# Second branch projection with eight of sixteen k-tiles as seven products for eight, modulation block 5 in the scan's last part, three low parts of y by adding DMAs

## The chip, the cores and the metric

The kernel runs on one core of a Trainium2 chip. The metric is the device time of one execution in microseconds (us), the median of three runs.

## What is computed

One step of a hybrid encoder layer for two groups of requests, 512 prompt frames and 64 sample frames, which share all weights (T = 576 rows together). The layer has a sparse attention branch and a Mamba-2 branch; each is projected back to 1024 channels and gated, the sum goes through an output projection, and a SwiGLU feed-forward part follows. The part that the change is about:

```
mod = (jax.nn.silu(c) @ w_ada + b_ada)[:, None, :]
sh1, sc1, gt1, sh2, sc2, gt2 = jnp.split(mod, 6, axis=-1)
...
y = (y.astype(x.dtype) + d_skip[:, None] * xh).reshape(b, t, D_INNER) * jax.nn.silu(z)
y = rms_normalize(y.reshape(b, t, SSM_GROUPS, D_INNER // SSM_GROUPS)).reshape(b, t, D_INNER) * g_ssm_norm
g_attn, g_ssm = jnp.split(jax.nn.sigmoid(gate_logits), 2, axis=-1)
mixed = (g_attn * (o_attn @ w_branch_attn) + g_ssm * (y @ w_branch_ssm)) @ w_out
x = x + gt1 * mixed
h2 = rms_normalize(x) * g_norm_ffn * (1.0 + sc2) + sh2
```

`o_attn` has 1024 columns, `y` has 2048. `w_ada` has 6 x 1024 columns; the kernel works on it in 12 blocks of 512 columns, and block u gives half of the u // 2-th of the six vectors (4 and 5: gt1; 6 and 7: sh2; 8 and 9: sc2; 10 and 11: gt2).

## The kernel before

**Numbers.** Every float32 operand of a large product is split into a high part (rounded to the format that TensorE multiplies fast, "float32r") and a low part, the rest. A product is hi·hi + hi·lo + lo·hi, three matmuls. ScalarE writes the high part (`wh`, `yh`, `mh`), VectorE subtracts it for the low part (`wl`, `yl`, `ml`). In 23 places GpSimd does it by an adding DMA instead: ScalarE writes the negative of the high part, and the DMA adds the raw value onto it (`split`, `by_dma`).

**Layout.** Activations lie with channels on the 128 partitions and the 576 rows in the free dimension, in two halves of TH = 288 (256 prompt rows and 32 sample rows in later stages). One matmul multiplies a 128 x 128 weight tile with 128 x 288 activations. A column block is 128 output channels. PSUM has the tag `mm` (two tiles of two banks), `px` and `py` (two banks each).

**Order of stages.** Input projection, attention, the scan of the Mamba-2 branch over eight channel groups g (`stage_a`, `stage_b`, `stage_c`), first branch projection (`pba`, eight column blocks of 8 k-tiles, attention), second branch projection (`pbs`, eight column blocks of 16 k-tiles, y), output projection (`pwo`), feed-forward part, of which most is computed with Strassen's method in Winograd's form: seven products of quarter matrices in place of eight, with sums of weight quarters (T1 to T4) and of activation quarters (S1 to S4).

**Scan, last part.** In the last groups the scan is a chain of short steps on all engines; matmuls of the first projection stand between them. `stage_c` of a group ends with y times its norm, written to DRAM (`y_d`), from which `load_split` (L1553) brings 128 x 576 tiles back into `stage` buffers and splits them. The last group's y stays in `ykeep`.

**Second projection** (L1620 to L1631). `gs` is the gate of a column block, `m` the gated first branch, which was written to DRAM (`m_d`). After the 96 matmuls of a block VectorE computes (gate + 1) times the product out of PSUM, adds `m`, ScalarE takes the high part `mh`, VectorE the low part `ml`, which the output projection reads.

**Modulation.** `ada_columns` (L792) multiplies 512 columns of `w_ada` with the two conditioning vectors on VectorE: per block 2 instructions of one operand, 14 that also add (tile `aacc`), on four loads of 512 KB (`adr`). `ada_sum` then adds over the partitions with 8 small matmuls and a transpose. Blocks 5 to 9 stand with low priority beside the second projection.

**What sets the order.** The kernel first records every operation and then a planner (`Plan.order`) puts them in order for each engine, by list scheduling: it has a cost for each kind of operation, buffers (`bufs`), priorities (`R.prio`, more is earlier) and a slack that it keeps between a producer and a matmul (`R.slack`). The engines then run that order strictly; an instruction whose input is late holds up all behind it on its engine, and SyncE's and GpSimd's DMA queues are such orders too. Weights are loaded (`raw`, 2 buffers) and split (3 buffers of `wh` and `wl`) ahead of their use by `fetch` (L628), and taken by `getw` (L657). All instructions have the line of the recording layer, so the profile is read by tile names.

Of the kernel before, what the change touches and what calls it, by code (L numbers as in the profile page):

```python
# [248 lines left out]
class Plan:  # L249
# [39 lines left out]
    def add(self, eng, fn, args, kw):  # L289
# [20 lines left out]
        op.dur, op.dur_dma = self.cost(op, outs, ins)  # L310
        self.ops.append(op)
# [240 lines left out]
def build(tc, I, O):  # L552
# [62 lines left out]
    queue = []  # L615
    state = {"ld": 0, "sp": 0, "get": 0}
    raws, outs, outs_made = {}, {}, []
# [9 lines left out]

    def fetch(done, limit=1 << 30):  # L628

        while len(outs_made) < len(specs):  # L630
            i = len(outs_made)
            outs_made.append(i)
            queue.extend((i, s) for s in specs[i])
            outs[i] = []
        with R.prio(4000 if done else 0):
            more = True
            while more:
                more = False
                j = state["ld"]
                if j < min(len(queue), limit) and j < state["sp"] + NRAW:  # L640
                    i, s = queue[j]
                    if s == "misc":
# [4 lines left out]
                    else:  # L647
                        raws[j] = (load_raw(*s), s[1], s[2], 27 <= j < 48)
# [3 lines left out]
                if j < min(state["ld"], limit) and (j < NWH or queue[j - NWH][0] < done):  # L652
                    outs[queue[j][0]].append(split(*raws.pop(j)))
                    state["sp"] += 1
                    more = True
# [87 lines left out]
    def ada(u, pl, bufs):  # L743

        p = px(f"pada{u}", "py")
        raws = [pl.tile([P, 2, 512], F32, name=f"wada{u}_{k2}", tag="adr", bufs=bufs) for k2 in range(4)]
        loads = [sync.dma_start(raw, w_ada[256 * k2:256 * k2 + 256, 512 * u:512 * u + 512].rearrange("(k p) n -> p k n", p=P))
                 for k2, raw in enumerate(raws)]
        with R.after(loads[-1:]):
            for kt in range(8):  # L750
                for g in range(4):
                    pe.matmul(p[32 * g:32 * g + 32, 0:P], sil[:, kt, :], raws[kt // 2][:, kt % 2, P * g:P * g + P],
                              start=(kt == 0), stop=(kt == 7), tile_position=(0, 32 * g))
        ada_out(u, p)

# [36 lines left out]
    def ada_columns(u, pl, nacc=1, bufs=2, nk=2, tags=None, late=False):  # L792

        acc = [pl.tile([P, 512], F32, name=f"aacc{u}{s}", tag=tags[s] if tags else f"aacc{s}", bufs=nacc) for s in range(2)]
        for k0 in range(0, 8, nk):
            raw = pl.tile([P, nk, 512], F32, name=f"wada{u}_{k0}", tag=tags[2 + k0 // nk % 2] if tags else "adr", bufs=bufs)
            (pool if u == 10 else sync).dma_start(raw, w_ada[P * k0:P * (k0 + nk), 512 * u:512 * u + 512].rearrange("(k p) n -> p k n", p=P))
            for j in range(nk):
# [8 lines left out]
        ada_sum(u, acc, px(f"padc{u}"))  # L807
# [550 lines left out]
    oh = [op_.tile([P, T], F32R, name=f"oh{k}") for k in range(8)]  # L1358
    ol = [op_.tile([P, T], F32R, name=f"ol{k}") for k in range(8)]
# [189 lines left out]
    def keep_split(o, hi, lo):  # L1549
        act.activation(hi, o, AF.Copy)  # L1550
        vec.tensor_tensor(lo, o, hi.bitcast(F32), OP.subtract)

    def load_split(pl, src, hi, lo, bufs):  # L1553
        o = pl.tile([P, T], F32, name="st_" + hi.base.name, tag="stage", bufs=bufs)
        sync.dma_start(o, src)
        keep_split(o, hi, lo)
# [701 lines left out]
```

## Time and profile before

| | us |
|---|---|
| median of three runs | 1356.81 (1356.64 to 1356.99) |
| profiled execution, its own time | 1357.67 |
| its span, first to last instruction | 1355.7 |

In a profile, each engine's busy time is counted from the start of its instructions to their end. PE is TensorE's matmuls, PEld its weight loads, DVE VectorE, ACT ScalarE, POOL GpSimd, SP SyncE. A group of instructions has a line `out<-in`, its shapes, count, busy time and mean nanoseconds, then the idle time of the engine just ahead of it and what ended that. In a list of waits the numbers are total, count and longest. A row of the chain has start, length, engine and tile. The busy shares in 40 slices of the run:

```profile
PE   7999999999999999999999999999999999999998
DVE  5788999887778798888887688867799999878897
ACT  5445333777777666666565342225476666665453
POOL 2312011230310235545463300001000000000000
DMA  9762435574755464454445698747423343325352
```

One slice is 33.9 us. The second branch projection lies in slices 24 to 27, where GpSimd has next to nothing to do and ScalarE is the least busy.

### The profile page before, as it was taken

The page shows a single profiled execution, that of the slowest core. Times are in us where ns is not written, and L with a number is a line of the kernel's source. Part 1 is how long each engine was busy: PE and PEld are TensorE (multiplying, and loading weights), DVE is VectorE, ACT ScalarE, POOL GpSimd, SP SyncE. Part 2 cuts the span into 40 slices and gives each one's busy share as a digit, 9 for nine tenths or more (in the row PEclk, how much of TensorE's full clock was granted, in tenths as well). Part 3 has the DMA queues.
Part 4 walks back from the last instruction along what each step waited for, and adds up shares of the span by engine and source line. Part 5 has one row for each costly group of instructions (what it writes and reads, how often), then busy time and mean ns, then how long its engine had stood idle before and what let it go on. Part 6 is the DMA issues. An engine that isn't in the chain of part 4 may idle for free.

```text
span 1355.7 us, 27900 instructions
## 1 busy us (share of the span) xinstructions
PE 1341.3 (99%) x10677; PEld 1306.5 (96%) x10677; DVE 1141.8 (84%) x2307; ACT 754.1 (56%) x1593; POOL 245.4 (18%) x377
## 2 busy tenths in 40 slices
PE   7999999999999999999999999999999999999998
PEld 6999999999999999999999999999999999999998
DVE  5788999887778798888887688867799999878897
ACT  5445333777777666666565342225476666665453
POOL 2312011230310235545463300001000000000000
PEclk9999999999999999999999999999999999999999
DMA  9762435574755464454445698747423343325352
GB/s 302 226 181 83 111 107 156 124 186 106 173 136 123 131 180 115 113 150 128 131 124 172 209 294 253 232 141 246 127 87 101 96 131 102 94 74 141 98 164 63
DMA packets 267877, 200.31 MB, mean 148 GB/s; under 512 B 25488, under 2 KB 239616, under 8 KB 267744
## 3 DMA queue, kind: packets, MB, share of 16 engines
q1 hardware_dynamic: 263056, 183.40, 46.3%
q0 software_dynamic: 4400, 15.00, 5.4%
q8 instruction: 83, 1.36, 0.4%
q14 instruction: 50, 0.41, 0.1%
q10 hardware_dynamic: 288, 0.13, 0.0%
HBM read 157.75 MB, written 28.96 MB: 138 GB/s over the span
## 4 chain that ended last, share of the span: by engine, by line
PE 91%; DVE 5%; DMA 1%; issue 1%; ACT 1%; POOL 1%; SPq 0%; DVEq 0%; POOLq 0%; ACTq 0%
PE mm L544 63%; PE py L544 16%; PE px L544 12%; DVE score L544 1%; DVE m L544 1%; DMA raw<-in_w_in 1%; DVE wl L544 1%; DMA bc<-acs_d 0%; DMA B<-in_w_down 0%; SPq L544 0%; DVE tok L544 0%; DVE xs L544 0%; ACT wh L544 0%; DVE rr L544 0%; ACT wl L544 0%
## 5 line engine op out<-in xcount | busy, mean ns | idle before, releaser
L544 ACT ACTIVATE wh<-raw 128x1024 fp32r<-128x1024 f32 (+3 forms) x144 | 140.6, 979 | 172.5 <-PE mm L544 131.6
L544 PE MATMUL mm<-hTl,wh 128*128 128x288 f32 (+1 forms) x1024 | 232.6, 302 | 1.1 <-DVE hTl L544 1.1
L544 PE MATMUL mm<-hTh,wh 128*128 128x288 f32 (+1 forms) x1024 | 231.2, 303 | 0.6 <-ACT wh L544 0.5
L544 PE MATMUL mm<-hTh,wl 128*128 128x288 f32 (+1 forms) x1024 | 230.0, 302 | 0.0
L544 PEld LDWEIGHTS mm<-hTl,wh 128*128 128x128 f32 (+1 forms) x1024 | 166.7, 188 | 4.1 <-DVE hTl L544 1.8
L544 PEld LDWEIGHTS mm<-hTh,wh 128*128 128x128 f32 (+1 forms) x1024 | 165.7, 188 | 3.8 <-ACT wh L544 0.7
L544 PEld LDWEIGHTS mm<-hTh,wl 128*128 128x128 f32 (+1 forms) x1024 | 165.4, 188 | 1.6 <-issue 0.9
L544 DVE TENSOR_TENSOR wl<-raw,wh 128x1024 fp32r<-128x1024 f32 (+2 forms) x99 | 122.1, 1235 | 27.1 <-ACT wh L544 26.0
L544 POOL DMA_DIRECT2D wl<-raw x23 | 20.9, 907 | 471.2 <-PE px L544 312.9
L544 DVE SCALAR_TENSOR_TENSOR cu<-xc,wc,cu 128x579 f32<-128x579 f32 x96 | 83.3, 868 | 2.0 <-ACT cu L544 1.0
L544 PE MATMUL mm<-wh,hTl 128*128 128x256 f32 x256 | 73.2, 286 | 0.0
L544 PE MATMUL mm<-wl,hTh 128*128 128x256 f32 x256 | 72.5, 284 | 0.0
L544 PE MATMUL mm<-wh,hTh 128*128 128x256 f32 x256 | 72.4, 285 | 0.0
L544 DVE SCALAR_TENSOR_TENSOR aacc<-adr,sil,aacc 128x512 f32<-128x512 f32 x84 | 59.0, 751 | 5.0 <-DMA adr<-in_w_ada 4.9
L544 PE MATMUL mm<-yh,wl 128*128 128x288 f32 x256 | 55.2, 296 | 0.0
L544 PE MATMUL mm<-yh,wh 128*128 128x288 f32 x256 | 55.0, 296 | 0.0
L544 PE MATMUL mm<-yl,wh 128*128 128x288 f32 x256 | 54.9, 296 | 0.0
L544 PE MATMUL mm<-xhS,wh 128*128 128x290 f32 (+1 forms) x248 | 54.8, 296 | 0.0
L544 ACT ACTIVATE P<-lg,mn 128x128 f32<-128x128 f32 (+4 forms) x72 | 41.7, 580 | 22.6 <-DVE mn L544 21.3
L544 ACT ACTIVATE dec<-dec,nacs 128x128 f32<-128x128 f32 x128 | 42.4, 393 | 15.9 <-POOL dec L544 15.9
L544 PE MATMUL mm<-xhS,wl 128*128 128x290 f32 (+1 forms) x232 | 51.2, 296 | 0.0
L544 PEld LDWEIGHTS mm<-wh,hTl 128*128 128x128 f32 x256 | 48.3, 189 | 0.4
(565 smaller groups left out, 4071.7 us busy)
## 6 DMA issues: line engine op xcount, KB each, us to landing
raw<-in_w_in SPq DMA_DIRECT2D x80, 512.0 KB, 4.2
adr<-in_w_ada SPq DMA_DIRECT2D x36, 512.0 KB, 5.4
raw<-in_w_gate_up SPq DMA_DIRECT2D x22, 512.0 KB, 3.8
wl<-raw POOLq DMA_DIRECT2D x21, 512.0 KB, 4.7
rawu<-in_w_gate_up SPq DMA_DIRECT2D x20, 512.0 KB, 3.9
bc<-acs_d SPq DMA_DIRECT2D x32, 256.0 KB, 3.7
raw<-in_w_branch_ssm SPq DMA_DIRECT2D x16, 512.0 KB, 4.7
gate_d<-sg SPq DMA_DIRECT2D x16, 288.0 KB, 2.2
```

What stands on the lines that cost most here:

```text
L544: getattr(engines[x.eng], x.fn)(*[real(a) for a in x.args], **{k: real(v) for k, v in x.kw.items()})
```

## The change

**Second projection.** Of y's 16 k-tiles the first eight (groups 0 to 3 of the scan) are cut in four quarters, by halves of the k-tiles and halves of the rows (A11, A12, A21, A22), and the weights of two neighbouring column blocks in quarters as well (B11 to B22). Such a pair of column blocks, here called a group r = 0 to 3, takes seven products of 4 k-tiles, 12 matmuls each, in the order `SSM_ORDER`. The sums of y quarters are made once; two of them and two quarters replace the operands of the first projection in their buffers (`oh`, `ol`) as soon as those have been read. The sums of weight quarters are made for each group in place, in the raw tiles. The other eight k-tiles are added as plain products: for the group's first column onto the banks `y` and `z`, in which products 2, 7 and 4 already lie, for its second onto `x` (which has products 1, 6, 5 and 3) and a new bank `w`. Copies of product 1, of 1 + 6 and of 7 are taken by ScalarE (`acc0`, `acc1`) while `x` and `z` go on collecting, so product 6 must wait until product 1 has been copied.

**Merge.** The gated first branch is added onto the gate's tile by a DMA from `m_d`. For the first six columns the low part `ml` is made by an adding DMA, for the last two by VectorE.

**Others.** The splits of y's tiles 8, 9 and 10 take their low part by an adding DMA. Modulation block 5 runs in the scan's last part, its sum ahead of the last `stage_c`; blocks 6 to 9 stay beside the second projection, with three load buffers and another PSUM tag; block 10's sum comes later, after the output projection. The planner counts some DMAs as longer by 2 or 4 us (`R.reserve`).

```diff
+    def pair_spec(w, r, names):
+        for i, q in enumerate(names):
+            specs.append([("quad", w, r, q, i == 0)])
+    def quad_source(key, pl, q):
+        b = pair_raws[key]
+        if "T2" not in b and q in ("T2", "T3"):
+            b["T1"], b["T3"] = b["B12"], b["B11"]
+            b["T2"] = pl.tile([P, 4, P], F32, name=f"T2b{key}", tag="T2b", bufs=1)
+            vec.tensor_tensor(b["T1"], b["B12"], b["B11"], OP.subtract)
+            vec.tensor_tensor(b["T2"], b["B22"], b["T1"], OP.subtract)
+            vec.tensor_tensor(b["T3"], b["T2"], b["B11"], OP.subtract)
+        if q == "T4":
+            b["T4"] = b["B21"]
+            vec.tensor_tensor(b["T4"], b["B21"], b["T2"], OP.subtract)
+        return b[q]
...
-    for a in range(8):
-        fm_spec(I["w_branch_ssm"][0], P * a, 0)
-        fm_spec(I["w_branch_ssm"][0], P * a, 1024)
+    SSM_ORDER = ((1, 2, 6, 7, 5, 4, 3),) + ((1, 7, 6, 2, 5, 4, 3),) * 3
...
+            with R.prio(-1000):
+                acc5 = ada_columns(4 + NADX, a5p, late=True, bank="py", bufs=2)
...
-    for k in range(16):
+    for k in range(8, 16):
         if k < 14:
-            load_split(gtp, y_d[:, k, :], yh[k], yl[k], 4)
+            load_split(gtp, y_d[:, k, :], yh[k], yl[k], 3, k in (8, 9, 10))
...
-        ps = fm(f"pbs{a}", getw(2), lambda k: yh[k], lambda k: yl[k])
-        vec.scalar_tensor_tensor(t2(g), t2(g), 1.0, ps, op0=OP.add, op1=OP.mult)
-        vec.tensor_tensor(m, m, g, OP.add)
+    def merged(a, parts):
+        g = gates[a]
+        for c0, n, ps in parts:
+            vec.scalar_tensor_tensor(g[:, c0:c0 + n], g[:, c0:c0 + n], 1.0, ps, op0=OP.add, op1=OP.mult)
...
+            pool.dma_start(g, m_d[:, a, :], accum_op=OP.add)
...
             act.activation(t2(mh[a])[:, :, d0:d0 + dn], src, AF.Copy)
-            vec.tensor_tensor(t2(ml[a])[:, :, d0:d0 + dn], src, t2(mh[a].bitcast(F32))[:, :, d0:d0 + dn], OP.subtract)
+            if a < 6:
+                act.activation(t2(ml[a])[:, :, d0:d0 + dn], t2(mh[a].bitcast(F32))[:, :, d0:d0 + dn], AF.Copy, scale=-1.0)
+                pool.dma_start(t2(ml[a])[:, :, d0:d0 + dn], src, accum_op=OP.add)
...
+        for p in SSM_ORDER[r]:
+            (hi, lo), = getw()
+            o, (yh_q, yl_q), starts = bank["y" if p == 2 else "z" if p in (7, 4) else "x"], yq[SSM_QUADS[p][1]], p in (1, 2, 7)
+            for k in range(4):
+                for w, y in ((hi, yh_q), (hi, yl_q), (lo, yh_q)):
+                    pe.matmul(o, w[:, k], y[:, k], start=(starts and k == 0 and w is hi and y is yh_q), stop=(k == 3 and w is lo),
+                              skip_group_check=not starts)
+            with R.prio(4000):
+                if p in (1, 6, 7):
+                    act.activation({1: acc0[:, :TH], 6: acc0[:, TH:], 7: acc1}[p], o, AF.Copy)
+                if p == 5:
+                    vec.tensor_tensor(acc1, acc1, o, OP.add)
...
-    with R.prio(-2000):
-        for u in range(4 + NADX + NADA, 10):
-            ada_columns(u, adv)
+    with R.prio(-2000):
+        for u in range(5 + NADX, 10):
...
+                ada_columns(u, adv, bank="py", bufs=3)
```

**Where instructions stand.** On TensorE before, in the middle of a column block of the second projection (`mm` is the product's bank pair, `yh`, `yl` the halves of y in float32r, `wh`, `wl` those of the weights, `aacc` and `ra` belong to a modulation block's sum):

```order
L544 MATMUL mm_114<-yh_0_9059,wl_104 128x288 x2
L544 MATMUL mm_114<-yh_0_9060,wh_101 128x288 x2
L544 MATMUL mm_114<-yl_0_9076,wh_101 128x288 x2
L544 MATMUL mm_114<-yh_0_9060,wl_104 128x288 x2
L544 MATMUL mm_115<-yh_0_9045,wh_102 128x288 x2
L544 MATMUL mm_115<-yl_0_9061,wh_102 128x288 x2
L544 MATMUL px_112<-aacc_0_9038,pick_120 32x128 x4
```

On TensorE after the change, at the start of group 1 (`yhA`, `ylA` and `yhS`, `ylS` are quarters of y and sums of them; `oh_0_5046` now holds a sum; both parts of a weight quarter lie in one tile, `wl_105` for product 1):

```order
L545 MATMUL mm_114<-ylA_0_9129,wl_105 128x288
L545 MATMUL mm_114<-yhA_0_9128,wl_105 128x288
L545 MATMUL px_113<-oh_0_5046,wh_103 128x288 x12
L545 MATMUL mm_115<-yhA_0_9130,wh_101 128x288
L545 MATMUL mm_115<-ylA_0_9131,wh_101 128x288
L545 MATMUL mm_115<-yhA_0_9130,wh_101 128x288
L545 MATMUL mm_114<-yhS_0_9132,wl_106 128x288
L545 MATMUL mm_114<-ylS_0_9133,wl_106 128x288
```

Where a block's matmuls ran straight through their 96, product 1 (`mm_114`) is now followed by the 12 of product 7 and three of product 2, and then by product 6 on product 1's bank.

On ScalarE before, beside the second projection (`mh` is the high part of the merged column):

```order
L544 ACTIVATE wh_103<-raw_99 128x1024
L544 ACTIVATE wh_101<-raw_100 128x1024
L544 ACTIVATE mh_0_9328<-m_9349 128x2x256
L544 ACTIVATE mh_0_9328<-m_9349 128x2x32
L544 ACTIVATE wh_102<-raw_99 128x1024
```

On ScalarE after, at the same start of group 1 (`acc` are the copies out of product banks, `rawp` the raw weights of a plain part):

```order
L545 ACTIVATE wl_104<-raw_99 128x512
L545 ACTIVATE mh_0_9384<-g_9403 128x2x256
L545 ACTIVATE acc_0_9107<-mm_114 128x288
L545 ACTIVATE wl_105<-raw_99 128x512
L545 ACTIVATE ml_0_9392<-mh_0_9384 128x2x256
L545 ACTIVATE acc_0_9108<-px_113 128x288
L545 ACTIVATE wh_103<-rawp_9100 128x1024
```

The merged column's `mh` now stands ahead of the copy of product 1 (`acc_0_9107<-mm_114`) in ScalarE's order; before, no copy of a product was made there.

On VectorE after, in the scan's last group (`xb`, `dec`, `xdt` belong to the scan, `g` to the first projection's gate):

```order
L545 SCALAR_TENSOR_TENSOR xb_5063<-xb_5063,dcol_87,py_111 128x128 x2
L545 TENSOR_SCALAR aacc_0_8526<-adr_8528,sil_119 128x512
L545 TENSOR_TENSOR dec_5069<-dec_5069,px_113 128x512
L545 SCALAR_TENSOR_TENSOR g_8512<-g_8512,mm_115 128x576
L545 TENSOR_SCALAR aacc_0_8527<-adr_8528,sil_119 128x512
L545 TENSOR_TENSOR wl_104<-raw_99,wh_101 128x1024
```

The two `aacc` instructions, and 14 more further on, are modulation block 5, which stood beside the second projection before.

More of the change, by code (lines that the diff above doesn't have):

```diff
@@ L651, in fetch @@
                 j = state["sp"]
[L652 to L655, printed above, removed]
+                free = lambda tag: len(slots[tag]) < NWH or slots[tag][-NWH] < done
+                if j < min(len(preps), limit) and preps[j][2] <= state["ld"]:
+                    i, quad, n = preps[j]
+                    if quad is None and free("wh") and free("wl"):
+                        outs[i].append(split(*raws.pop(n - 1)))
+                        for tag in slots:
+                            slots[tag].append(i)
+                        state["sp"] += 1
+                        more = True
+                    tag = ("wh", "wl")[state["half"] % 2]
+                    if quad is not None and free(tag):
+                        r, q = quad
+                        if n - 2 in raws:
+                            x, y = (raws.pop(n - 2 + k)[0] for k in range(2))
+                            pair_raws[r] = {"B11": x[:, 0:4], "B21": x[:, 4:8], "B12": y[:, 0:4], "B22": y[:, 4:8]}
+                        src = quad_source(r, sum_pool[0], q)
+                        t = wp.tile([P, 8, P], F32R, name=f"wq{q}{r}", tag=tag, bufs=NWH)
+                        act.activation(t[:, 0:4], src, AF.Copy)
+                        vec.tensor_tensor(t[:, 4:8], src, t[:, 0:4].bitcast(F32), OP.subtract)
+                        outs[i].append((t[:, 0:4], t[:, 4:8]))
+                        slots[tag].append(i)
+                        state["half"] += 1
+                        state["sp"] += 1
+                        more = True
     def getw(n=1):
@@ L741, in build @@
     sh1, sc1, gt1, sh2, sc2, gt2 = (modc[:, i] for i in range(6))
[L743 to L754, printed above, removed]
     pairs_bank = px("padp", "py")
@@ new lines, in build @@
+    yh, yl = ({k: yh_p.tile([P, T], F32R, name=f"y{n}{k}") for k in range(8, 16)} for n in "hl")
+    yq = {q: [yh_p.tile([P, 4, TH], F32R, name=f"y{n}{q}") for n in "hl"] for q in ("A11", "A12", "S2")}
+    src = {}
+    for i, q in enumerate(("A11", "A12", "A21", "A22")):
+        with R.prio(1500):
+            src[q] = gtp.tile([P, 4, TH], F32, name=f"yr{q}")
+            R.reserve = 2
+            sync.dma_start(src[q], y_d[:, 4 * (i % 2):4 * (i % 2) + 4, TH * (i // 2):TH * (i // 2) + TH])
+            R.reserve = 0
@@ L1720, in build @@
             operand(f"A{hf + 1}{j // 2 + 1}", j % 2, y2[j, hf])
+    m = px("pad10")
+    ada_sum(10, acc10, *(m[:, k * P:k * P + P] for k in range(2)))
     def late_operand(q):
```

158 lines of the change are left out of this document (126 added, 32 removed).

## The prediction

> **What bounds the kernel now.** I read the busy times first, then the waits of TensorE, then the stage of the second branch projection by itself.
>
> ```profile
> span 1355.7 us, 27900 instructions
> PE 1341.3 (99%) x10677; PEld 1306.5 (96%) x10677; DVE 1141.8 (84%) x2307; ACT 754.1 (56%) x1593; POOL 245.4 (18%) x377
> PE 91%; DVE 5%; DMA 1%; issue 1%; ACT 1%; POOL 1%; SPq 0%; DVEq 0%; POOLq 0%; ACTq 0%
> PE py L544 <- POOL ident L544: 1.7, 1, 1.7
> PE py L544 <- DVE xwS L544: 0.5, 1, 0.5
> core 0: 1355.7 us, clock 0.999
> ```
>
> TensorE (PE) is busy for 99% of the span and holds 91% of the chain that ended last. Because a matmul's end is modelled, busy PE alone proves little; the waits do. The fourth row is PE's longest wait in the whole run (1.7 us, at the very start). The fifth is the only row in the list of PE's waits for the stretch from 690 to 911 us, in which the scan ends and both branch projections run: 0.5 us. The granted clock is full. So a matmul taken out there shortens the run, and a wait put in lengthens it.
>
> ```profile
> L544 PE MATMUL mm<-yh,wh x256: 291/294/378, 804.7 to 910.2; 128*128 128x288 f32 x128
> L544 PE MATMUL mm<-yh,wl x256: 288/294/401, 805.2 to 910.8; 128*128 128x288 f32 x128
> L544 PE MATMUL mm<-yl,wh 128*128 128x288 f32 x256 | 54.9, 296 | 0.0
> 899.89 46.38 PE mm L544 x348
> 1256.35 4.79 PE px L544 x36
> ```
>
> The second projection is 768 matmuls of 288 columns, from 804.7 to 910.8 us. The 294 ns are the latency of one. What counts is the spacing: the chain has 348 of them in 46.38 us, 133.3 ns each. The 768 take 102.4 us; the other 3.7 us of the stage are the five sums of modulation blocks 5 to 9, about 0.75 us each. The last row is a stretch of the down projection, which already runs as seven products for eight: 36 matmuls in 4.79 us, 133.1 ns. The new form, where one operand quarter follows another instead of two halves sharing a weight, costs the same per matmul.
>
> **The change, part by part.** *Matmuls.* Of the 16 k-tiles, eight stay plain: 8 column blocks x 8 k-tiles x 3 x 2 halves = 384. The other eight become 4 pairs of column blocks x 7 products x 4 k-tiles x 3 = 336. Together 720 for 768: 48 fewer, **-6.4 us**. PE does no fewer modulation sums: block 5's goes into the scan, block 9's behind the first output-projection column, the rest stay. That moves 0.75 us twice and saves nothing.
>
> *VectorE in this stage.* The prices:
>
> ```profile
> 804.50:831.00 26.50, 26.50 (x212) 26.13 (x211) 24.07 (x38) 6.97 (x9) 0.00 (x0) 1.00 0.93 304
> 831.00:858.00 27.00, 27.00 (x224) 26.48 (x226) 22.48 (x35) 6.64 (x9) 0.00 (x0) 1.00 0.77 237
> 858.00:884.00 26.00, 26.00 (x219) 25.44 (x212) 23.35 (x40) 4.95 (x8) 0.00 (x0) 1.00 0.72 220
> 884.00:911.00 27.00, 27.00 (x215) 26.64 (x214) 15.31 (x24) 5.91 (x9) 1.60 (x6) 1.00 0.48 144
> L544 DVE SCALAR_TENSOR_TENSOR aacc<-adr,sil,aacc 128x512 f32<-128x512 f32 x70 | 48.5, 744 | 1.0 <-DMA adr<-in_w_ada 0.9
> L544 DVE TENSOR_SCALAR aacc<-adr,sil 128x512 f32<-128x512 f32 x10 | 4.6, 478 | 0.0
> L544 DVE TENSOR_TENSOR wl<-raw,wh 128x1024 fp32r<-128x1024 f32 x24 | 29.5, 1228 | 8.7 <-ACT wh L544 8.5
> L544 DVE TENSOR_TENSOR wh<-raw,wh 128x512 fp32r<-128x512 f32 x13 | 8.8, 678 | 0.0
> L544 DVE TENSOR_TENSOR T<-rawu 128x512 f32<-128x512 f32 x11 | 7.5, 680 | 0.0
> L544 DVE SCALAR_TENSOR_TENSOR g<-g,mm 128x576 f32<-128x576 f32 x8 | 6.0, 751 | 7.4 <-PE mm L544 7.2
> L544 DVE TENSOR_TENSOR m<-m,g 128x576 f32<-128x576 f32 x8 | 6.0, 756 | 0.2
> L544 DVE TENSOR_TENSOR ml<-m,mh 128x512 fp32r<-128x512 f32 x8 | 5.5, 682 | 0.0
> L544 DVE TENSOR_TENSOR ml<-m,mh 128x64 fp32r<-128x64 f32 x8 | 1.7, 216 | 0.0
> L544 DVE TENSOR_TENSOR gg<-u,py 128x288 f32<-128x288 f32 x9 | 4.0, 440 | 0.0
> L544 DVE TENSOR_TENSOR yl<-stage,yh 128x576 fp32r<-128x576 f32 x14 | 10.1, 753 | 0.5 <-ACT yh L544 0.5
> 822.14 4.06 DVE L544 SCALAR_TENSOR_TENSOR aacc<-adr,sil,aacc 128x512 f32<-128x512 f32 x6
> ```
>
> In the four windows (columns after the length: PE, PEld, DVE, ACT, POOL busy, clock, DMA share, GB/s) VectorE is busy 24.07 + 22.48 + 23.35 + 15.31 = 85.2 of 106.5 us. Away go eight merging adds (8 x 0.756 = 6.0), six low parts of the merged columns (6 x 0.898 = 5.4), modulation block 5 (14 x 0.744 + 2 x 0.478 = 11.4) and eight of sixteen weight splits (8 x 1.228 = 9.8). New are 28 quarter splits (28 x 0.678 = 19.0), 16 weight sums (16 x 0.68 = 10.9), 16 adds out of PSUM (16 x 0.44 = 7.0) and some late splits of y (two of 1152 columns, 1.36 each by the line through 576 and 1024 columns, and one more of 0.753: 3.5). The net is +7.8, so 93 of about 100 us. That is too high rather than too low: six instructions of 744 ns took 4.06 us, each overlapping the next by 0.08. VectorE stays below PE, but with little to spare, and it takes no part of the saving unless one of its inputs comes late.
>
> *Block 5 in the scan.* 11.4 us of VectorE go to where the page's second part and the windows leave it free:
>
> ```profile
> 738.00:756.00 18.00, 11.01 (x24) 1.00 0.82 257
> 756.00:772.00 16.00, 10.92 (x25) 1.00 0.48 154
> 772.00:788.00 16.00, 9.17 (x18) 1.00 0.71 223
> ```
>
> 31.1 busy of 50 us (the second number; then clock, DMA share and GB/s). The scan's short steps can each wait for at most one block instruction (0.744 us), while the first projection's matmuls keep PE fed. Cost 0; without that cover up to 0.7 per step. Its 2 MB of loads also leave the stretch that follows.
>
> *Low parts by adding DMAs, and the merge.* They need GpSimd to issue 23 DMAs, and ScalarE copies ahead of them:
>
> ```profile
> L544 POOL DMA_DIRECT2D wl<-raw x23 | 20.9, 907 | 471.2 <-PE px L544 312.9 <-ACT wl L544 123.4 <-ACT tok L544 19.1
> DMA to landing us min/median/max: 3.9/4.7/7.0
> m<-m_d SPq DMA_DIRECT2D x8, 288.0 KB, 4.4
> L544 ACT ACTIVATE mh<-m 128x512 fp32r<-128x512 f32 x8 | 5.1, 634 | 9.1 <-DVE m L544 9.1
> L544 ACT ACTIVATE t<-mm 128x290 f32<-128x290 f32 x20 | 8.3, 414 | 13.9 <-PE mm L544 13.9
> ```
>
> 23 x 0.907 = 21 us of an engine that was busy 1.6 us in the stage. What matters is a queue. In groups 1 and 3 ScalarE has to take the merged column's high part (`mh<-g`, which waits for an adding DMA) *before* it copies product 1 out of its bank, and product 6 adds onto that bank. From the last matmul of the earlier column, PE has 48 + 12 + 12 + 3 = 75 matmuls until product 6: 10.0 us. The chain: two adds 0.88, three half-width splits and sums 2.04, the gate 0.75 (3.3 with the overlaps), the DMA 4.7, `mh` 0.634, the copy 0.414, some 0.3 of hand-overs: 9.4. Slack 0.6. With the longest landing (7.0) product 6 waits 1.7 us, twice in the stage: bounds 0 and 3.4. The nearest rows (4.7 on the same queue, 4.4 for the same size) lie at the lower end; I take 0.8. At the stage's end the last column's chain (VectorE 3.5, DMA 4.7, `mh` 0.87, low part 0.68 and hand-overs: 10.1) stands against 78 matmuls and one modulation sum (11.2), so 0, and 1.2 with the longest landing. At the start, product 7 needs the split of the third quarter 60 matmuls (8.0 us) after column 6's end, and VectorE has 7.6 us of work at most before it: 0, up to 2 if a load is late.
>
> On DMA load a rule can be weighed. The windows show the 16 DMA engines 93% busy just when the stage begins and 48% at its end. The Trainium skill says in "DMA: Bandwidth & Descriptors", section "Issuing engines are not separate DMA queues", that transfers issued by GpSimd run on the same 16 engines as SyncE's and interleave with them. By it nine more transfers of 288 KB (2.65 MB) cost, at the 304 GB/s of the fullest window, an estimated 8.7 us of DMA time, which the 29 us idle in the windows can hold, so the sum stays; it speaks for late landings rather than against the saving.
>
> **Sum.** -6.4 + 0.8 = -5.6 us. The profiled execution took 1357.67 us (span 1355.7), so 1352.1; it lies 0.86 above the median of the runs, 1356.81, which becomes **1351.2**.
>
> **Rivals.** *A: landings near 7 us.* Then 3.4 + 1.2 + up to 2 come back: some 5 of the 6.4, so 1355.4, within the measurement's resolution (about 0.2%, 2.7 us). For it speaks the DMA share of 0.93; against it that adding DMAs landed in 4.7 us in the median.
>
> *B: slower, by the loop of the two gate buffers.* The gate of column a + 2 is loaded into the buffer that column a's low part is read from, by an adding DMA behind another one. From a group's end: VectorE 2.7, DMA 4.7, ScalarE 1.3, another issue ahead in GpSimd's queue 0.9, 4.7 to landing, then the load:
>
> ```profile
> g<-gate_d SPq DMA_DIRECT2D x16, 288.0 KB, 3.4
> stage<-y_d SPq DMA_DIRECT2D x14, 288.0 KB, 5.9
> ```
>
> Together 2.7 + 4.7 + 1.3 + 0.9 + 4.7 + 3.4 = 17.7 us. VectorE needs the gate some 20.5 us after the group's end (132 matmuls, two adds and three splits): slack 2.8. With 7.0 for both adds and 5.9 for the load the chain is 7.1 longer, VectorE stands 4.3 us, and having under a tenth of its time free it passes that on to PE: three group boundaries, 13 us, less the 6.4 gained: 1363.4. It decides for slower from (6.4 + 2.7) / 3 = 3.0 us per boundary, that is when the chain is 5.8 longer. Against it: three long landings in a row, each time. By the Trainium skill ("TensorE: Matmul & The Clock Gate", section "HAM oscillation — how this bites in real kernels"), a PE gap above about 3.4 us drops the matmul clock for a while; an estimate from its figures is 0.8 us more per gap, 1366. No run here shows such a gap: the longest wait is 1.7 us and the clock full.
>
> *C: more than the matmuls.* PE's 0.5 us of waiting in the scan goes too and nothing waits: 1349.9, down to 1349.3 with the spread of the runs.
>
> *D: no saving.* The 720 matmuls might run slower, as the plain part of a group's first column now alternates between two banks of different tiles; at 142 ns each the saving is gone: 1357. The down projection's 133.1 ns speaks against it.
>
> **Chances.** Forecast (0 to 2.7 us given back, 1350.4 to 1353.1) 0.64; C 0.10; A 0.18, one third of it still faster; B 0.06; D 0.02. So faster 0.64 + 0.10 + 0.06 = 0.80, same 0.12 + 0.02 = 0.14, slower 0.06. The range leaves out B, the far half of A and the edge of C: **1349.6 to 1355.6**.
>
> **What would show it.** The rows of y's matmuls should add up to 720 at 133 ns, and the stage should be about 100 us less what PE waits. A shows as PE waiting for ScalarE's `acc` in groups 1 and 3, with `mh` waiting for DMA; B as VectorE waiting for `g<-gate_d`; D as matmuls spaced over 133 ns. The forecast is wrong if PE's waits between the first projection and the output projection exceed 3 us in all, or if stages outside this stretch change by over 1 us.

## The result, and the profile after

The changed kernel took 1366.29 us (median of 6 runs, 1364.24 to 1371.46) beside 1357.38 for the kernel before: ratio 1.0069, 95% interval 1.0051 to 1.0087. It is 9 us slower; the forecast was 1351.2, 6 us faster, with a range up to 1355.6. Of the variants below, one of the six runs of e5 took 2212.6 us in a slow state, and it is left out of e5's median (1362.3 with it) and ratio.

The profiled execution is the slowest of the six (1371.46 us, span 1369.7), some 5 us above their median, so single waits in it are read together with those of the variants below. From its page (busy lines, chain, DMA queues):

```profile
span 1369.7 us, 27930 instructions
PE 1343.6 (98%) x10629; PEld 1305.0 (95%) x10629; DVE 1165.4 (85%) x2343; ACT 773.0 (56%) x1639; POOL 275.6 (20%) x400
q1 hardware_dynamic: 262864, 181.04, 45.4%
q0 software_dynamic: 9248, 20.02, 7.9%
PE 75%; DVE 11%; DMA 6%; issue 5%; ACT 2%; POOL 1%; SPq 0%; DVEq 0%; POOLq 0%; ACTq 0%
```

The 48 matmuls are gone (10,629 for 10,677), and yet TensorE holds 75% of the chain in place of 91%: more of it now runs through other engines and DMAs, for which TensorE waits. The largest in the list of TensorE's waits over the whole span, without one of 1.7 us at the very start (engine and tile, what it waited for, total, times, longest):

```profile
PE mm L545 <- ACT acc L545: 3.7, 2, 1.9
PE py L545 <- DVE xw L545: 2.2, 2, 2.0
PE mm L545 <- ACT mh L545: 1.7, 1, 1.7
PE mm L545 <- ACT wh L545: 1.5, 2, 1.1
```

Before, from the first projection to the end of the output projection ("the stage" below: first `oh` matmul to last `mh` or `ml` matmul), TensorE waited 0.5 us; now 7.9. And behind three of these waits stands a second loss. Two rows around the wait at 842 us, and one around that at 817 us (length; PE, PEld, DVE, ACT, POOL busy; granted clock, DMA share, GB/s):

```profile
840.00:842.50 2.50, 0.74 (x5) 0.50 (x4) 0.04 (x1) 1.21 (x3) 0.54 (x1) 1.00 1.13 349
842.60:845.90 3.30, 3.30 (x16) 3.30 (x15) 3.13 (x5) 2.57 (x7) 1.22 (x1) 0.50 0.71 167
818.70:821.90 3.20, 3.20 (x15) 3.20 (x15) 3.20 (x7) 0.11 (x1) 0.00 (x0) 0.50 0.82 216
```

TensorE idles for most of 2 us, and right behind that the clock is granted at 0.50 for some 3.4 us: 16 matmuls in 3.3 us. Each such stretch costs 1.7 us more, so a wait of 1.8 us costs 3.5.

Three places account for the difference of the two profiled spans, 14.0 us: the first projection begins at 741.6 us in place of 738.4 (3.2), the stage takes 234.0 us in place of 225.7 (8.3), what follows it 2.5 more. Of the stage, 7.9 us are waits and 5.1 the half clock; the rest is 221.0, against 225.2 before worked out the same way. So 4.2 of the 6.4 us are there, and 12.5 us are lost beside them.

How two of these waits come about stands in the timeline (start, duration, engine, instruction, and in brackets what ended its idle time):

```profile
815.12 2.15 ACT L545 ACTIVATE yh<-stage 128x576 fp32r<-128x576 f32 x3 [2.74 <-DMA stage<-y_d]
817.17 0.39 ACT L545 ACTIVATE acc<-mm 128x288 f32<-128x288 f32 x1
817.61 2.44 PE L545 MATMUL mm<-ol,wh 128*128 128x288 f32 x12 [1.89 <-ACT acc L545]
...
834.05 0.87 POOL L545 DMA_DIRECT2D g<-m_d  x1 [28.41 <-DVE g L545]
...
841.29 0.63 ACT L545 ACTIVATE mh<-g 128x512 fp32r<-128x512 f32 x1 [4.83 <-DMA g<-m_d]
841.82 0.39 ACT L545 ACTIVATE acc<-mm 128x288 f32<-128x288 f32 x1
```

The adding DMA of the merge lands 7.2 us after its issue; ScalarE stands at `mh`, and behind it waits the copy of product 1, which product 6 of the next group needs. In group 0 it is another copy, that of products 1 + 6, which product 5 needs (`ol` holds its operand): at 815 us it stands behind copies of y whose loads are late. The list of DMA issues has the median landings (last column, us):

```profile
g<-m_d POOLq DMA_DIRECT2D x8, 288.0 KB, 6.7
yl<-stage POOLq DMA_DIRECT2D x3, 288.0 KB, 7.4
```

And the windows of the stage:

```profile
808.00:831.00 23.00, 20.88 (x144) 20.41 (x143) 21.77 (x32) 11.04 (x17) 0.00 (x0) 0.93 0.82 247
831.00:858.00 27.00, 25.24 (x189) 24.64 (x188) 21.34 (x37) 8.34 (x18) 6.57 (x6) 0.94 0.81 200
858.00:884.00 26.00, 25.69 (x204) 25.09 (x202) 21.26 (x38) 9.58 (x21) 5.40 (x5) 1.00 0.87 210
884.00:917.00 33.00, 31.93 (x247) 31.16 (x248) 30.33 (x49) 11.50 (x22) 8.72 (x8) 1.00 0.97 234
```

The DMA engines, which went down to 0.48 at the end of the second projection before, are now at 0.81 to 0.97 to its end, and mostly at fewer GB/s than the 237 to 304 of before's two fullest windows.

### The profile page after: what moved, and what is told of

Its sections match the earlier page's. It is cut to its first block, busy times and chain, and to the rows that moved or that the text cites. A ratio compares the mean times of both kernels' runs of the same rounds, so it can differ in the third digit from the quotient of the medians.

```text
span 1369.7 us, 27930 instructions
## 1 busy us (share of the span) xinstructions
PE 1343.6 (98%) x10629; PEld 1305.0 (95%) x10629; DVE 1165.4 (85%) x2343; ACT 773.0 (56%) x1639; POOL 275.6 (20%) x400
## 3 DMA queue, kind: packets, MB, share of 16 engines
q1 hardware_dynamic: 262864, 181.04, 45.4%
## 4 chain that ended last, share of the span: by engine, by line
PE 75%; DVE 11%; DMA 6%; issue 5%; ACT 2%; POOL 1%; SPq 0%; DVEq 0%; POOLq 0%; ACTq 0%
PE mm L545 48%; PE py L545 15%; PE px L545 11%; DVE score L545 3%; DMA g<-m_d 2%; DVE m L545 2%; DVE wl L545 1%; DMA zt<-z_d 1%; DMA raw<-in_w_in 1%; DVE aacc L545 1%; DMA T<-in_w_ada 0%; ACT wh L545 0%; SPq L545 0%; DMA bc<-acs_d 0%; DMA g<-gate_d 0%
## 5 line engine op out<-in xcount | busy, mean ns | idle before, releaser
L545 PE MATMUL mm<-hTl,wh 128*128 128x288 f32 (+1 forms) x1024 | 234.0, 303 | 1.1 <-DVE hTl L545 1.1
L545 ACT ACTIVATE wh<-raw 128x1024 fp32r<-128x1024 f32 (+3 forms) x140 | 130.9, 938 | 119.6 <-PE mm L545 82.4
L545 DVE TENSOR_TENSOR wl<-raw,wh 128x1024 fp32r<-128x1024 f32 (+2 forms) x83 | 102.6, 1238 | 13.2 <-ACT wh L545 11.9
L545 PEld LDWEIGHTS mm<-wh,hTh 128*128 128x128 f32 x256 | 48.1, 188 | 0.6 <-issue 0.4
L545 PEld LDWEIGHTS mm<-wl,hTh 128*128 128x128 f32 x256 | 48.3, 188 | 0.2
L545 DVE CUSTOM_DVE_ANT_0 lg<-py,mask 128x128 f32<-128x128 f32 (+4 forms) x72 | 33.9, 483 | 15.2 <-PE py L545 15.0
```

Of the source, the lines that this page charges most:

```text
L545: getattr(engines[x.eng], x.fn)(*[real(a) for a in x.args], **{k: real(v) for k, v in x.kw.items()})
```

## The experiments

Each theory's numbers were written before its run. "Waits", "half clock" (length of the stretches at 0.5) and "rest" (stage less waits less half of that part of the half clock that lies outside waits) are for the stage, in us, from the profiled execution of each run. e6, e7 and e11 leave out part of the modulation's work or loads, so they are for measuring only.

| run | edit | median | ratio (95%) | stage | waits | half clock | rest |
|---|---|---|---|---|---|---|---|
| before | | 1357.38 | 1 | 225.7 | 0.5 | 0 | 225.2 |
| after | | 1366.29 | 1.0069 (1.0051-1.0087) | 234.0 | 7.9 | 10.2 | 221.0 |
| e1 | merge by VectorE, 2 buffers | 1366.75 | 1.0073 (1.0059-1.0087) | 231.3 | 10.1 | 6.8 | 219.8 |
| e2 | y's low parts by VectorE | 1366.38 | 1.0072 (1.0059-1.0085) | 229.0 | 5.2 | 3.4 | 222.1 |
| e3 | block 5 back | 1373.78 | 1.0131 (1.0117-1.0145) | 239.2 | 13.4 | 10.2 | 222.7 |
| e4 | planner: adding DMAs 3 us later | 1397.73 | 1.0301 (1.0286-1.0315) | 244.0 | 16.6 | 17.1 | 220.9 |
| e5 | scan order back | 1361.50 | 1.0040 (1.0027-1.0053) | 229.0 | 6.4 | 3.4 | 220.9 |
| e6 | half the sums | 1362.67 | 1.0045 (1.0033-1.0057) | 225.3 | 4.4 | 3.4 | 219.2 |
| e7 | half the loads | 1359.65 | 1.0021 (1.0013-1.0030) | 224.3 | 3.9 | 0 | 220.3 |
| e8 | e5, no adding DMA, 2 buffers | 1366.78 | 1.0078 (1.0065-1.0091) | 233.4 | 10.7 | 10.2 | 220.7 |
| e9 | e5, only the merge by DMA | 1364.15 | 1.0059 (1.0047-1.0071) | 231.8 | 7.5 | 6.8 | 220.9 |
| e10 | e5, no products | 1364.26 | 1.0065 (1.0051-1.0080) | 233.7 | 5.5 | 3.4 | 226.4 |
| e11 | e5, half of both | 1353.75 | 0.9972 (0.9960-0.9984) | 221.0 | 2.3 | 0 | 218.8 |
| e12 | e5, one block early | 1398.82 | 1.0303 (1.0282-1.0324) | 229.6 | 7.8 | 3.4 | 220.0 |
| e13 | e12, no adding DMA, 2 buffers | 1392.88 | 1.0263 (1.0249-1.0277) | 223.6 | 3.9 | 0 | 219.7 |
| e14 | e5, 2 buffers | 1366.80 | 1.0079 (1.0066-1.0093) | 234.6 | 11.3 | 10.2 | 220.5 |
| e15 | e5, product 2 ahead of 6 | 1360.55 | 1.0026 (1.0014-1.0037) | 228.7 | 6.7 | 3.4 | 220.2 |
| e16 | e15, last merge by VectorE | 1359.25 | 1.0025 (1.0014-1.0036) | 227.0 | 5.6 | 3.4 | 219.7 |
| e17 | e16, turns 6 us later | 1358.59 | 1.0013 (1.0004-1.0022) | 226.2 | 4.8 | 3.4 | 219.6 |
| e18 | e16, turns 4 us later, more slack in group 0 | 1361.49 | 1.0032 (1.0020-1.0045) | 230.8 | 8.0 | 6.8 | 219.9 |

The last column has most of the answer: with the seven products it is 219 to 223 everywhere, without them 225 or 226. What else differs from run to run is mostly waits and half clock.

### First round: which part makes the waits (e1 to e4)

```diff
-            if a >= 8:
+            if a >= 0:          # e1: m loaded, added by VectorE; adr bufs=3 -> 2
-            load_split(gtp, y_d[:, k, :], yh[k], yl[k], 3, k in (8, 9, 10))
+            load_split(gtp, y_d[:, k, :], yh[k], yl[k], 3, k in ())          # e2
-        for u in range(5 + NADX, 10):
+        for u in range(4 + NADX, 10):          # e3, and acc5 out of the scan
+        op.dur_dma += 3.0 if eng == "gpsimd" and kw.get("accum_op") is not None else 0          # e4
```

> Undone: the adding DMA of the merge. The first branch's half is loaded into a tile again and VectorE adds it (8 adds of 0.756 us; modulation weights get two buffers instead of three, to make room). Theory Q (queue): ScalarE stands in order at a copy that waits for an adding DMA (7.2 us from issue to landing), TensorE's accumulator copies stand behind it, and each wait of 1.7 to 1.9 us is followed by 3.4 us at half clock, worth 1.7 us more. Then the waits of 1.76, 1.06 and 1.73 us go, and the half clock behind two of them: 4.6 + 3.4 = 8 us in the profiled execution, and a time of 1358 to 1361 us. Theory V (VectorE is the bound, about 93% of the stage): 6 us more work for it, 1368 to 1372 us, TensorE waiting for VectorE. Theory L (block 5's loads in the scan delay other loads): no change, 1366 us.

> Undone: the three low parts of y by adding DMAs; VectorE subtracts them (3 x 0.75 us). Theory Q: the staging buffers come free at a landing 7.4 us after the add's issue, so the next y tile is loaded late, ScalarE stands at its copy and product 1's accumulator copy stands behind it. That wait (1.89 us) and the half clock behind it (1.7 us) go: 1362 to 1364 us. Theory V: 2.3 us more of VectorE, 1367 to 1369 us. Theory L: 1366 us.

> Undone: modulation block 5 in the scan; its loads and its 11.4 us of VectorE stand beside the second projection again. Theory Q: the same waits for the adding DMAs, 1364 to 1369 us. Theory V: VectorE would need more than the stage has, at least 5 us more: 1371 us or more. Theory L: the scan's 2.0 us wait and the late loads go: 1361 to 1363 us.

> No instruction changes: only the planner counts 3 us more until an adding DMA lands, so that it may put other copies ahead of those that wait for one. Theory Q: the accumulator copies come ahead of the merged column's copy, and the waits for ScalarE shrink to under 0.6 us: 1357 to 1361 us. Theory V: no change beyond 2 us, 1366 us. Theory L: no change, 1366 us.

None of the first three brought the time that theory Q asked for (in e2 the wait at the second projection's start became one of 1.6 us for VectorE's `yl`). Theory L fits e1 and e2 but falls by e3, for which it asked for 1361 to 1363 us. e4 lost 31 us: its edit also reached the adding DMAs of earlier stages, the first projection began at 751.0 us, and TensorE waited 4.4 and 4.7 us for `g`. It says that the planner's orders are brittle and little else. e1 is the telling one. TensorE's longest waits in its stage:

```profile
PE py L545 <- DVE aacc L545: 4.4, 2, 4.2
PE mm L545 <- DVE x L545: 3.8, 1, 3.8
PE py L545 <- DVE hst L545: 1.1, 1, 1.1
PE mm L545 <- ACT acc L545: 0.7, 1, 0.7
```

The wait for `mh` is gone and those for `acc` are down to 0.7, as Q said; in their place TensorE stands for VectorE, 4.4 us for block 9's sums and 3.8 for `x`, with a half clock. e3 shows that moving block 5 was worth some 8 us to this kernel (1.0131 against 1.0069): theory V's price, though not its whole story.

### Second round: the scan's order, and room (e5 to e7)

All of e1 to e4 kept a wait of 1.6 or 1.7 us for `xw` in the scan, at about 662 us (672 in e4), where the change has 2.0. In the kernel after, the timeline there is:

```profile
651.96 0.36 SPq L545 DMA_DIRECT2D bc<-acs_d  x1
652.42 0.45 SPq L545 DMA_DIRECT2D raw<-in_w_in  x1
652.96 0.53 SPq L545 DMA_DIRECT2D bc<-acs_d  x1
...
658.90 0.41 POOL L545 TENSOR_SCALAR_AFFINE_SELECT decS<-bc 64x256 f32<-64x256 f32 x1 [6.09 <-DMA bc<-acs_d]
659.35 0.59 ACT L545 ACTIVATE decS<-decS,nacs 64x64 f32<-64x64 f32 x2 [5.26 <-POOL decS L545]
...
660.92 1.23 DVE L545 TENSOR_TENSOR wl<-raw,wh 128x1024 fp32r<-128x1024 f32 x1 [2.28 <-ACT wh L545]
662.29 0.42 DVE L545 TENSOR_TENSOR xw<-px,wst 128x256 f32<-128x256 f32 x1 [0.15 <-ACT bt L545]
```

A weight load of 512 KB now stands between the two small `bc` loads; the second lands 5.9 us after its issue, GpSimd, ScalarE and VectorE pass it on, and `xw` comes late. The order there changed because `load_split` adds the planner's reserve of 2 us to every load it makes, and the scan uses it for the attention output too.

```diff
-        R.reserve = 2
+        R.reserve = 2 if bufs == 3 else 0          # e5: only y's loads
-            for j in range(nk):
+            for j in range(1 if 6 <= u <= 9 else nk):          # e6
+            nl = 1 if 6 <= u <= 9 else nk          # e7: raw[:, 0:nl] loaded, raw[:, j % nl] read
```

> Undone: only the reserve of 2 us that the planner adds to each load of load_split, for the eight loads of the attention output in the scan; with it gone every engine's order up to TensorE's 5,537th matmul (about 740 us) is that of before. In all variants so far TensorE waits 1.6 to 2.0 us for xw at about 662 us and the first projection starts 2.0 to 3.2 us later than before. Theory S (the reserve reorders the scan): that wait goes, the first projection starts within 0.6 us of before's 738.4, and the time is 1363.5 to 1364.5 us. Rival (a late landing that any order meets): 1366 us and the wait stays.

> Leaves out half of the products of modulation blocks 6 to 9 on VectorE (32 x 0.744 = 23.8 us of its work); all their loads, 512 KB each, stay. Theory V (VectorE falls behind, its work and the in-order stalls together fill the stage): TensorE's waits between the first projection and the end of the output projection shrink from 5 to 8 us to under 1.5 us: 1357 to 1359 us. Theory Q (ScalarE's copies stand behind adding DMAs): the waits for acc and mh stay, 1363 to 1366 us. Theory D (the DMA engines are too full, 82 to 97% of the windows): 1364 to 1366 us.

> Leaves out half of the bytes of modulation blocks 6 to 9: each load brings 256 KB instead of 512, and VectorE does both products from the same row, so its work is the same. 4 MB of some 45 MB go in the stage. Theory D: landings get shorter and the waits shrink: 1358 to 1361 us. Theory V: 1365 to 1367 us. Theory Q: the adding DMAs land about 1 us earlier, 1363 to 1365 us.

e5 puts the two `bc` loads next to each other again, the `xw` wait goes, the projection begins at 737.5 us, and the kernel gains 4 us (1.0069 to 1.0040): theory S, and more than it asked for. In e5's row of the same place:

```profile
648.76 0.95 SPq L545 DMA_DIRECT2D bc<-acs_d  x2
```

e6 gains about 3.5 us and e7 about 6.5, each with the scan's wait still in it: neither VectorE's time (V) nor the DMA engines' (D) is the only thing short, though e7's time lies within theory D's 1358 to 1361 and e6's not within V's. In e6 the waits for `acc` stay (3.5 us in all, theory Q), in e7 they are down to 0.5.

### Third round: adding DMAs or products (e8 to e10, e14)

```diff
-            if a < 6:
+            if a < 0:          # e8, e9: low parts of the merged columns by VectorE
-        ps = [pmm(f"pbs{r}{i}") for i in range(2)]
...
+        for a in (2 * r, 2 * r + 1):          # e10: 16 plain k-tiles, as before
+            ps = fm(f"pbs{a}", getw(2), lambda k: yh[k], lambda k: yl[k])
+            merged(a, ((0, T, ps),))
-                ada_columns(u, adv, bank="py", bufs=3)
+                ada_columns(u, adv, bank="py", bufs=2)          # e14, and in e1, e8, e13 for room
```

> e5 (scan order back, 1362.3 us) with none of the three kinds of adding DMAs: the merge, the low parts of the merged columns and the three low parts of y all on VectorE (6.0 + 5.4 + 2.3 = 13.7 us more for it; modulation weights in two buffers for room). Theory A (the 23 adding DMAs fill the DMA engines and hold ScalarE's line): DMA share of 831 to 911 us falls from 0.93-0.96 to about 0.85, the waits for acc and mh (4.0 us) and the half clock (1.7) go: 1356 to 1359 us. Theory V (VectorE falls behind): TensorE waits for VectorE 8 us or more, 1366 us or more. If both hold, the time stays within 2 us of e5 and the waits change their name.

> e5 with only the merge's eight adding DMAs left: low parts of the merged columns and of y on VectorE (7.7 us more). Theory A: 15 of 23 adding DMAs gone, so landings of the other eight shorter than 5.8 us, 1359 to 1361 us. Theory V: 4 us or more slower than e5, 1366 us or more.

> e5 without the seven products: the projection's 768 matmuls as before, and the rest of the change as it is (block 5 in the scan, the 23 adding DMAs). Theory P (the products' own chain makes the waits: accumulator copies in ScalarE's line, quarter sums and splits on VectorE): no wait over 0.6 us in the stage, 1355.5 to 1358 us. Theory A: the adding DMAs' waits stay, at least 3 us, 1359 us or more.

> e5 with two buffers in place of three for the loads of modulation blocks 6 to 9, nothing else: the part that e1, e8 and e13 had to change for room. In e8 TensorE waited 6.8 us for block 9's sums, behind loads that waited for one of the two buffers. If the buffers made that wait (theory B), this kernel shows a wait for aacc of 3 us or more at about 925 us and 1365 to 1370 us. If VectorE's 13.7 us more made it (theory V), no such wait, 1361.5 to 1364 us.

e8 looks like theory V (6.8 us for `aacc`), but e14 has the same loss with all its adding DMAs: two buffers alone cost about 5 us over e5, by a wait at the same place. In e14 (theory B, if a little under its 3 us for `aacc`):

```profile
PE py L545 <- DVE ra L545: 3.7, 1, 3.7
PE py L545 <- DVE aacc L545: 2.8, 1, 2.8
```

So e1 and e8 had spoilt their own test, and the fair pair is e8 against e14, both with two buffers: 1366.78 and 1366.80. Taking all 23 adding DMAs away, at 13.7 us more of VectorE, changes nothing. e9 against e5 (three buffers in both) is 2.7 us slower by the medians, with intervals that just overlap. The adding DMAs cost no more than they save.

e10 was a surprise: the plain projection with the rest of the change is 2.8 us slower than e5. Its largest waits:

```profile
PE mm L545 <- DMA yl<-stage: 2.2, 1, 2.2
PE mm L545 <- DVE g L545: 1.5, 1, 1.5
```

The 2.2 us are an adding DMA that TensorE waits for itself, with a half clock behind it; the 1.5 us come from the two gate buffers, where VectorE stands for the gate:

```profile
836.95 0.75 DVE L545 SCALAR_TENSOR_TENSOR g<-g,mm 128x576 f32<-128x576 f32 x1 [2.81 <-DMA g<-gate_d]
```

So the extras of the change make waits even beside the plain projection (rest 226.4, waits 5.5). Theory P, that the products' own chain alone makes them, falls; which of e5's waits are due to the products is not settled. Between e10 and e5, with the same extras, the rest falls by 5.5 us: most of the 6.4.

### Fourth round: is it room (e11 to e13)

> e5 (scan order back) with half the products and half the bytes of modulation blocks 6 to 9 left out: 23.8 us less of VectorE, 4 MB less of loads; the 23 adding DMAs, the products and ScalarE's lines stay. Theory C (the saving is there, and is lost because VectorE and the DMA engines have no room beside the shorter stage): waits and half clock of the stage fall from 9.6 to under 2 us, 1351.5 to 1354.5 us. Theory Q (ScalarE's line behind adding DMAs makes them whatever the load): acc and mh waits of 3 us or more with a half clock stay, 1357 to 1361 us.

> e5 with one modulation block more done early: block 5 beside block 4 under the attention, block 6 in the scan, 7 to 9 beside the projection; nothing is left out. 11.4 us of VectorE and 2 MB of loads leave the stage. Theory C: between e5 and e11, 1356 to 1359 us, unless the attention loses what the stage gains (then its start shows it: the first projection would begin over 1 us after e5's 737.5). Theory Q: 1361 to 1363 us.

> e12 without any adding DMA (13.7 us more for VectorE, modulation weights in two buffers): what e8 is to e5. Theory V with e8's reading (there VectorE was 8 us late at the stage's end): with 11.4 us less to do it is no longer late, the wait for aacc (6.8 us) goes, 1356 to 1359 us. If VectorE's total is not what decides there, the aacc wait stays, 1364 us or more.

```diff
-NADX = 1
+NADX = 2          # e12, e13; and for u in range(4, 4 + NADX): ada_columns(u, adx, 1, 1, 1)
```

e11 is the first kernel with the products that beats the kernel before: 1353.75 us, ratio 0.9972, within theory C's 1351.5 to 1354.5. All its waits of over 0.2 us in the stage:

```profile
PE px L545 <- DVE oh L545: 1.8, 1, 1.8
PE mm L545 <- DVE acc L545: 0.4, 1, 0.4
```

No wait for `mh`, none for ScalarE's `acc`, no half clock, although all 23 adding DMAs and ScalarE's line are as in e5. It leaves out work, so it is no kernel to use; it shows that the saving comes out where there is room: its stage is 4.7 us shorter than before's. e12 tried to make that room honestly and failed elsewhere: TensorE waited 11.3 us under the attention for block 5's sums, with 17 us of half clock, and the first projection began at 775.6 us. That is the exception that its expectation allowed for, far larger than thought. e13, without adding DMAs, has no wait for `aacc` at the stage's end any more, as theory V had it for a stage with more room: its stage took 223.6 us, 2.1 less than before; but its time is lost under the attention as e12's is.

### Fifth round: the line behind one DMA (e15 to e18)

```diff
-    SSM_ORDER = ((1, 2, 6, 7, 5, 4, 3),) + ((1, 7, 6, 2, 5, 4, 3),) * 3
+    SSM_ORDER = ((1, 2, 6, 7, 5, 4, 3),) + ((1, 7, 2, 6, 5, 4, 3),) * 3          # e15
+            mixed[7] = [(0, adv.tile([P, 4 * P], F32, name="m7a", tag="T2b", bufs=1)), (4 * P, mxt.tile([P, T - 4 * P], F32, name="m7b"))]          # e16
-            R.slack = SLACK
+            R.slack = 6.0 if 6 <= u <= 9 else SLACK          # e17 (4.0 in e18), ahead of ada_out
+        R.slack = 2.5 if r == 0 else 0.8          # e18, group 0 of the products
```

> e5 with product 2 ahead of product 6 in groups 1 to 3: 12 matmuls (1.6 us) more between product 1 and product 6, which waits for ScalarE's copy of product 1. Theory Q: the wait for acc of 1.5 us at about 835 us goes or falls under 0.3, no new one over 0.6: 1360 to 1361.5 us. Rival (product 2's bank comes free too late, or the planner shifts the wait): same time as e5 within 1 us, 1361.5 to 1363.5.

> e15 with the last column's merge on VectorE (0.9 us of work) and not by an adding DMA; the seven others stay. Theory Q: the wait for mh at the start of the output projection (1.78 us in e5) and the half clock behind it (1.7) go: 3 to 3.5 us faster than e15, 1357 to 1358.5 us. Theory V: VectorE is late at that point whatever adds, the wait changes its name, within 1 us of e15.

> e16 with 6 us of slack, in place of 0.25, that the planner gives TensorE before it turns the modulation sums of blocks 6 to 9: in e16 TensorE waited 2.8 us for VectorE's copy ra, behind a split that waited for ScalarE, which waited for an adding DMA; then half clock. No instruction is added. Theory Q: the line behind the adding DMA stays, but nothing of TensorE stands in it: the wait goes and the half clock with it, 3 to 4.5 us faster than e16, 1355 to 1357 us. Rival (TensorE meets the same late VectorE at the next thing it needs): within 1 us of e16, 1358.5 to 1360 us.

> e16 with 4 us of slack for the turns, and in group 0 with product 6 behind product 7 (12 matmuls, 1.6 us later): in e16 product 6 waited 1.7 us there for the copy of product 1, which stood in ScalarE's line behind copies of y that waited for late loads. Theory Q: that wait goes too: 1 to 2 us faster than e17. Rival (product 7's own operands are late at that place): no gain on e17, a wait for the third quarter's operand in place of acc.

The waits that e15 and e16 were aimed at, in e5:

```profile
PE mm L545 <- ACT acc L545: 2.3, 3, 1.5
PE mm L545 <- ACT mh L545: 1.8, 1, 1.8
```

In e15 the wait for `acc` at 835 us went and one of 2.4 us for `ra` came; the median lies in theory Q's range, but only 1 us below e5's, with overlapping intervals, so nothing is decided. The 1.8 us for `mh` at the output projection was already gone in e15's profile, where the last merge landed in 4.5 us; e16 had nothing left to take away there, `ra` stayed with 2.8, and the ratio is that of e15. Behind that `ra` stands the same line, in e16:

```profile
867.68 0.63 ACT L545 ACTIVATE mh<-g 128x512 fp32r<-128x512 f32 x1 [4.61 <-DMA g<-m_d]
868.22 0.61 ACT L545 ACTIVATE wl<-raw 128x512 fp32r<-128x512 f32 x1
...
868.86 0.69 DVE L545 TENSOR_TENSOR wl<-raw,wl 128x512 fp32r<-128x512 f32 x1 [5.07 <-ACT wl L545]
869.47 0.48 DVE L545 TENSOR_SCALAR aacc<-adr,sil 128x512 f32<-128x512 f32 x1
869.87 0.28 DVE L545 COPY ra<-py 128x128 f32<-128x128 f32 x1
```

One adding DMA holds ScalarE 4.6 us, ScalarE holds VectorE 5.1, VectorE holds TensorE. e17, which lets TensorE ask for `ra` later, then waited 2.2 us for VectorE's `acc`: it gained 0.7 us by the medians and 1.6 by the ratios, not 3 to 4.5. That is the rival. It is the best whole kernel with the products: 1358.59 us, ratio 1.0013 (1.0004 to 1.0022), 7 to 8 us faster than the change as it was made and still not faster than before. e18 did not do what its expectation says: TensorE's order in group 0 is that of e16, and the wait there, 1.4 us at 814 us, is product 5's for the copy of 1 + 6, as in e16; at 849 us it made a wait of 3.8 us of its own.

## Why the prediction was wrong

**The matmuls: right.** 48 fewer; the rest of the stage falls from 225.2 to between 218.8 and 222.7 us, 2.5 to 6.4 less for a forecast of 6.4. Rival D (slower matmuls) is out: in the plain part of group 0, 36 matmuls that take turns on two banks start 133 ns apart (825.74 to 830.40 us), and 49 of the products in group 2 also (865.10 to 871.47).

**The step that failed is the term of new waits, "I take 0.8", between bounds 0 and 3.4 for product 6.** In its place stand 7.9 us of waits in the profiled execution, and 6.4 in e5. The chain was worked out rightly: for a landing of 7.0 us it gave product 6 a wait of 1.7, and group 1 has a landing of 7.2 and a wait of 1.8 at 842 us; in group 3 the merge landed in 4.6 us and product 6 did not wait. What was wrong was the landing. I took 4.7, the median of adding DMAs in a kernel whose DMA engines had gaps; the medians in the change are 6.7 (merge) and 7.4 (y). At the end the landing was 7.2 and the wait 1.7 (forecast 0, up to 1.2). At the start the size fits (1.9, forecast 0, up to 2 if a load is late), but not the place: product 5 waited for the copy of 1 + 6, which the sum does not have, and not product 7 for its quarter. That is mostly rival A's mechanism, which I gave 0.18; its price of "some 5" is also less than the sum of its own bounds, 3.4 + 1.2 + 2 = 6.6.

**Why the landings were long: in part, it seems, the estimate of DMA time.** I took 2.65 MB at the rate of the fullest window, 8.7 us. By the queue lines, the adding queue went from 5.4% to 7.9% of the span, and the other one fell a little. Before, the page has:

```profile
q1 hardware_dynamic: 263056, 183.40, 46.3%
q0 software_dynamic: 4400, 15.00, 5.4%
```

So 5.02 MB more on the adding queue took 7.9% of 1369.7 less 5.4% of 1355.7, 35 us of all 16 engines, or 7.0 us a MB, against 3.4 on the other queue; net of 6 us saved there, 29 us, as much as the windows had idle. (It is the time of packets, which can overlap: one row above has a share of 1.13.) The rule cited in the prediction (in the Trainium skill, "DMA: Bandwidth & Descriptors", section "Issuing engines are not separate DMA queues") agrees with this; the price per byte was mine. That the fuller engines made the landings long is argued, not shown. The merge's landings in e6, which leaves out no bytes, and the merge's and y's in e11:

```profile
g<-m_d POOLq DMA_DIRECT2D x8, 288.0 KB, 5.1
g<-m_d POOLq DMA_DIRECT2D x8, 288.0 KB, 4.8
yl<-stage POOLq DMA_DIRECT2D x3, 288.0 KB, 7.4
```

The merge's got shorter with either kind of room, y's did not.

**Not in the sum at all: the half clock.** I let it stand with rival B alone, for gaps of over 3.4 us, as the Trainium skill has it in "TensorE: Matmul & The Clock Gate", section "HAM oscillation — how this bites in real kernels". Here waits of 1.6 to 2.2 us were followed by it, three times in the profiled execution: 5.1 us. Each cost 1.7 us, twice the 0.8 that the prediction estimated for a gap. The measurement decides.

**Not in the sum: the scan.** I wrote that stages outside the stretch changing by over 1 us would show the forecast wrong. The first projection begins 3.2 us later, and e5 puts 4 us of the loss down to the planner's reserve on loads that the change had no need to touch. I had read the reserve as part of the second projection.

**VectorE: half right.** It stays below TensorE in the windows, as forecast, and that says little: TensorE waits where VectorE stands in line for something else, with 14 of 109 us free on average (the four windows above).

**Rival B** ended on the right side for another reason. Its loop of gate buffers shows in e10 (VectorE waits of 2.1 to 3.8 us for the gate), where it costs TensorE 1.5 us once, not 13.

What adds up to the 15 us between forecast (1351.2) and median (1366.3): 4 to 5 by the scan's order (e5); the other 10, e5's 1361.5 less the forecast, are first its stage's waits, 6.4 and 1.7 of half clock where 0.8 stood. The rest are 2.1 in the stage's rest (220.9, where 225.2 less 6.4 is 218.8; its cause is open) and 1.5 in what follows it (393.1 for 391.6), less 0.9 by which the first projection starts earlier than before. By e11 some 8 to 9 us go when VectorE and the DMA engines get room. How that room divides between the two is not settled: e6 gave 3.5 and e7 6.5, and each edit also shifts the planner's order, so that a luckier order is not ruled out as part of it. After the stage, a wait of 0.6 to 2.4 us for `gg` in the down projection shows in the kernel after and in every variant but e10, and not before: it goes with the products, but I did not find how.

## What to carry to other kernels

When work is taken from the engine that bounds a stage, ask what the stage's other engines and its DMA queues have free in the new, shorter stage, and price a chain through a DMA by the landing under the load that the change itself makes, not by the median of before. In-order engines turn one late landing into a late everything: look for what stands behind the instruction that waits, on each engine in turn, and whether TensorE asks for any of it. After an edit to a planner's numbers, compare the order of every stage, also those that the edit is not about.

## What the runs showed of the hardware that was not expected

- Adding DMAs in pieces of about 1 KB (5.02 MB in 4,848 packets) took twice the DMA time per byte of plain ones: 7.0 us of all 16 engines a MB against 3.4, though the plain ones' pieces are smaller still (181.04 MB in 262,864). With more room, in e11 (q0 at 8.1% of 1352.5 us), it was 7.2, so the fuller engines did not make the price.
- The half clock came behind short waits. Of the single TensorE waits in the profiles (outside start and end), 1 of 43 between 1.0 and 1.6 us was followed within 3 us by 3.4 us at 0.50; of those from 1.6 to 2.2 us, 11 of 24; of two of 2.4 us (e2, e15), none; the 17 of 2.8 us or more all had one behind or beside them. A wait of 4.2 us (e1) had 6.8 us of it, one of 11.3 (e12) 17.1, which began within the wait.
